# 512- and 256-column matmuls with added halves in the q, k and first gate and value units of an encoder block

## The chip, the core and the metric

The kernel runs on one NeuronCore of a Trainium2 chip. The metric is the device time of one execution in microseconds; of several runs the median is taken. The engines named below: PE is TensorE (matmul; PEld are its weight loads), DVE is VectorE, ACT is ScalarE, POOL is GpSimd, SP is SyncE, which issues most transfers.

## The reference

One layer of a bidirectional encoder, 256 positions of 2048 features, everything in float32:

```python
h = rmsnorm(x, norm1_g)
q, k, v, u = split(h @ w_in)             # 12 q heads, 4 k and v heads of 128, u 512 wide
a = window_attention(q, k, v, sink)      # |t-s| <= 128, ALiBi, a sink logit for each head
f = fourier_mix(u, w_fourier)            # DFT over positions and channels, then a map per group
x = x + concat(rmsnorm(a), rmsnorm(f)) @ w_out
h = rmsnorm(x, norm2_g)
gate, val = split(h @ w_up)              # 5504 each: 43 tiles of 128
gate = conv3(gate) + dw_b                # depthwise over positions
y = rmsnorm(x + (gelu(gate) * val) @ w_down)
```

## The kernel before

Every large product is made of three: an operand is split into a high part (rounded to fp32r, the form that PE multiplies fast) and a low part (what the rounding left), and high x high, high x low and low x high are summed in PSUM. Weights come by DMA into `raw`, and `split` makes the parts: ACT copies the high half into a tile `parts`, DVE subtracts for the low half (L170, L171). `parts` has three buffers; `PLACES` says how many columns into the tile the two halves start. A unit's weights are split two units ahead.

The work is a row of units, written out by hand in the order in which each engine runs it; there is no scheduler. First u and v (weights stream, the activations are stationary), then 16 units of k and q (`QK_ORDER`: one k head, its three q heads, four times), the output projection, then gate and value tiles in pairs (`ups`). In the q, k, gate and value units the weights are stationary: for each of 16 slices of the contraction `still_weights` runs three matmuls of 256 columns into the same 256 columns of a PSUM bank. Their moving operand is `hT[k // 4][:, k % 4, :]`, 512 columns: the activations' high part in the first 256 (`h[:, 0:S]`) and the low part behind it:

```python
for n, (w, o) in enumerate([(hi, 0), (hi, S), (lo, 0)]):
    nc.tensor.matmul(ps[:, 0:S], w[:, s], h[:, o : o + S], ...)
```

After a unit its PSUM is read: k is scaled by `r1b` on DVE, q is split straight from PSUM (`qk_out`, `qk_parts`); a gate or value tile is scaled by `r2b` (`scaled_sum`), the gate goes through the convolution and GELU, and both are multiplied. Around a q or k unit lie the small matmuls of heads further on: scores, transposes and values (`before` a unit on PE, `beside` and `behind` it on ACT, DVE and POOL).

Gate and value units of the first eight tiles, and three more, run one after another: 19 units, the first two of them interleaved with transposes of x. From then on (`PATTERN`) they alternate with products of the down-projection (`by_parts`: 12 matmuls of 512 columns each). The last six gate and value units again run on end, between two blocks of down units of 96 matmuls of 512 columns.

Of the kernel before, what the change touches and what calls it, by code (L numbers as in the profile page):

```python
# [8 lines left out]
F32 = mybir.dt.float32  # L9
F32R = mybir.dt.float32r  # L10
AF = mybir.ActivationFunctionType
ALU = mybir.AluOpType

P = 128
D = 2048
S = 256
NK = D // P
# [46 lines left out]
def ff_items():  # L64


    def ups(tiles):
        return [(kind, j) for j in tiles for kind in ("gate", "val")]

    items = ups(range(8))  # L70
    for g in range(N_GROUPS):
        todo = {
            "u": ups(range(8 * g + 8, 8 * g + 16)),
            "s": [("product", g, c, p) for c in range(2) for p in PRODUCTS[c]],
        }
        items += [todo[c].pop(0) for c in PATTERN]
        assert not any(todo.values())
    items += [("down", 0, c) for c in range(4)] + ups(LAST)
    items += [("down", 1, c) for c in range(4)] + [("last", c) for c in range(4)]
    return items  # L80
# [3 lines left out]
def block_kernel(  # L84
# [18 lines left out]
    nc = tc.nc  # L103
# [10 lines left out]
    def bank(pool, name):  # L114
        return pool.tile([P, 512], F32, tag=pool.name, name=name)


    units = [(w_in[i], 2048, "first" if i < N_QK else "still") for i in range(24)]
    units += [(w_out[i], 2048, "moving") for i in range(16)]
    n_front = len(units)  # L120
    items, up_index = ff_items(), {}
    for n, it in enumerate(items):
        if it[0] == "product":
            continue
        up_index[n] = len(units)
        if it[0] in ("gate", "val"):
            units.append((w_up[2 * it[1] + (it[0] == "val")], 2048, "still"))
        elif it[0] == "down":
            units.append((w_down_late[4 * it[1] + it[2]], 2048, "moving"))
        else:  # L130
            units.append((w_down_last[it[1]], 512 * len(LAST), "moving"))
    RAW = 3
    raws, halves = {}, {}


    PLACES = {"still": (0, 32), "first": (16, 16), "moving": (0, 0), "product": (28, 28)}

    def parts_tile(name, place):
        t = wp.tile([P, 2 * 2048 + 128], F32R, tag="parts", name=name, bufs=3)
        oh, ol = PLACES[place]  # L140
        return t[:, oh : oh + 2048], t[:, 2048 + ol : 4096 + ol]
# [38 lines left out]
    ph = pa.enter_context(tc.tile_pool(name="pa", bufs=1))  # L180

    hT = []
# [19 lines left out]
    first = load(0, 4)  # L202
# [50 lines left out]
    ps = bank(dn, "ps_warm")  # L253
# [58 lines left out]
                ps, ah, wl, start=False, stop=last and q == q0 + len(kk) - 1  # L312
            )

    def still_weights(hi, lo, ps, kk):


        for k in kk:
            h = hT[k // 4][:, k % 4, :]
            s = slice(k * P, (k + 1) * P)  # L320
            for n, (w, o) in enumerate([(hi, 0), (hi, S), (lo, 0)]):
                nc.tensor.matmul(  # L322
                    ps[:, 0:S], w[:, s], h[:, o : o + S],
                    start=k == 0 and n == 0, stop=k == NK - 1 and n == 2,
                )
# [17 lines left out]
    before, beside, behind = {}, {}, {}  # L343

    def at(when, i, f, *a):
        when.setdefault(i, []).append((f, a))
# [17 lines left out]
    for k in range(NK):  # L364
        c, q = k // 4, k % 4
# [4 lines left out]
        hi, lo = halves[c]  # L370
# [49 lines left out]
    r1b = ph.tile([P, S], F32, tag="r1b", name="r1b")  # L420
# [137 lines left out]
    for c in range(4):  # L558

        def work(hi, lo):  # L560
            for b in range(2):
                moving_weights(
                    hi, lo, 512, range(4 * c, 4 * c + 4), hk, b, ps_v[b], c == 0, c == 3
                )
# [4 lines left out]
    qk_sb, st = {}, {}  # L569
    sq_a = ph.tile([P, S], F32, tag="sq", name="sq_a")  # L570

    def qk_out(kind, h):
        ps = st.pop(("ps", kind, h))[:, 0:S]
        if kind == "k":
            add = ph.tile([P, S], F32, tag="add", name=f"add_{kind}{h}", bufs=2)
            nc.vector.tensor_tensor(add, ps, r1b, ALU.mult)
            ps = add
        st["add", kind, h] = ps

    def qk_parts(kind, h):  # L580

# [99 lines left out]
    for i in range(N_QK, N_OUT + 8):  # L681
        heads = {i - s: h for (kind, h), s in slot_of.items() if kind == "q"}
        new = [kh for kh, s in slot_of.items() if i - s == 1]
        if 5 in heads:
            at(before, i, values, heads[5])
        if 4 in heads:
            at(before, i, turn, heads[4])
        if 2 in heads:
            at(before, i, scores, heads[2])
        if 3 in heads:  # L690
            at(beside, i, weigh, heads[3])
        for kind, h in new:
            at(beside, i, qk_out, kind, h)
        if 5 in heads:
            at(beside, i, values_out, heads[5])
        if 4 in heads:
            at(beside, i, turn_out, heads[4])
        for kind, h in new:
            at(beside, i, qk_parts, kind, h)
        if 2 in heads:  # L700
            at(beside, i, scores_out, heads[2])
            at(behind, i, exps, heads[2])

    fourier_channels_steps()
    for n, (kind, h) in enumerate(QK_ORDER):

        def work(hi, lo):
            ps = st["ps", kind, h] = bank(mm, f"ps_{kind}{h}")
            still_weights(hi, lo, ps, range(NK))

        unit(N_QK + n, work)

# [49 lines left out]
    for n, (c, kq) in enumerate(OUT_ORDER):  # L762
        i = N_OUT + n
# [14 lines left out]
        if kq >= 2:  # L778
            part = "a" if kq == 2 else "f"
            ps = ps_a[c] if kq < 3 else ps_a[c, "f"]  # L780
# [15 lines left out]
    fp = ctx.enter_context(tc.tile_pool(name="fp", bufs=2))  # L796
    hT[:] = hT2
    r2b = fp.tile([P, S], F32, tag="r2b", name="r2b", bufs=1)
    parts = {}
    gate_out, sums_of, act = {}, {}, {}  # L800

    def scaled_sum(ps, name):
        add = fp.tile([P, S], F32, tag="fadd", name=f"fa_{name}", bufs=3)
        nc.vector.tensor_tensor(add, ps[:, 0:S], r2b, ALU.mult)  # L804
        sums_of[name] = add

    def gate_conv(j):
# [139 lines left out]

    def up_posts(n, kind, j, ps):
        if kind == "gate":
            at(beside, n + 1, scaled_sum, ps, f"g{j}")  # L950
            at(beside, n + 2, gate_conv, j)
            at(behind, n + 2, gate_gelu, j)
        else:
            at(beside, n + 1, scaled_sum, ps, f"v{j}")
            at(beside, n + 2, val_mult, j)
            if j % 8 == 7 and j < 8 * N_GROUPS:
                g = j // 8
                at(behind, n + 1, operand, g, "P1")
                at(behind, n + 2, operand, g, "N4")
                at(behind, n + 3, operand_sums, g, 0)  # L960
                at(behind, n + 4, operand, g, "P7")
                at(behind, n + 4, operand, g, "P2")
                at(behind, n + 5, operand_sums, g, 1)
                at(behind, n + 5, operand, g, "N5")
                at(behind, n + 6, operand, g, "N3")
                at(behind, n + 7, operand, g, "P6")
            if j >= 8 * N_GROUPS:
                at(behind, n + 2, act_parts, j)
# [102 lines left out]
    for q in range(2):  # L1071
        kind, j = items[q]
        ps = bank(mm, f"ps_{kind}{j}")
# [15 lines left out]
    for n, it in enumerate(items):  # L1089
        if n < 2:  # L1090
            continue
        if it[0] == "last":
            break
        if n in (8, 9):
            ring_load()
        if n == 13:
            pending.append(lambda: first_sums(0, 0))
        if it[0] in ("gate", "val"):
            kind, j = it
            ps = bank(mm, f"ps_{kind}{j}")  # L1100
            still_weights(*halves.pop(up_index[n]), ps, range(NK))
            ff_step(n)
            up_posts(n, kind, j, ps)
            continue
        if it[0] == "product":
            kind, g, c, p = it
            end = g == N_GROUPS - 1
            if (c, p) in held:
                by_parts(held[c, p], parts[p], *halves.pop(it), g == 0, end)
            else:  # L1110
                ps = bank(mm, f"ps_{p}{g}{c}")
                by_parts(ps, parts[p], *halves.pop(it), True, True)
                at(beside, n + 1, product_out, g, c, p, ps)
            if end and p == "N4":
                at(behind, n + 1, shared_out, c)
        else:
            kind, g, c = it
            hi, lo = halves.pop(up_index[n])
            ps = [bank(mm, f"ps_l{g}{c}{b}") for b in range(2)]
            for b in range(2):  # L1120
                moving_weights(hi, lo, 512, LATE[g], act.get, b, ps[b], True, True)
            at(beside, n + 1, down_out, c, ps)
            if (g, c) == (0, 0):
                gfb = fp.tile([P, D], F32, tag="sumw", name="gfb", bufs=1)
                nc.gpsimd.dma_start(gfb, normf_g.partition_broadcast(P))
        ff_step(n)
# [3 lines left out]
    i = up_index[n]  # L1130
# [145 lines left out]
```

## Time and profile before

| | before |
|---|---|
| median of 3 runs | 959.62 us (959.04 to 959.85) |
| the profiled execution | 959.13 us |
| its span, first to last instruction | 957.4 us |
| PE, weight loads | busy 947.8 and 884.8 us |
| DVE, ACT, POOL | busy 703.0, 510.5 and 44.6 us |
| HBM | 208.65 MB read, 2.10 MB written |

The span is the time between the first and the last instruction on the core; the execution's own time holds some 1.7 us around it. Matmuls are pipelined: a row's duration is that of one matmul from its first operand to its modelled end (277 ns for 256 columns), and the pace is the distance between starts. The row of the chain of work that ended last gives a start, a length and the number of matmuls that it merged.

### The profile page before, as it was taken

How to read it: one execution, taken by the hardware profiler on the slowest of the kernel's cores; microseconds unless marked ns; L12 is line 12 of the kernel's file. 1: busy time of each engine (PE TensorE's matmuls, PEld its weight loads, DVE VectorE, ACT ScalarE, POOL GpSimd, SP SyncE). 2: the span in 40 equal slices, each digit the busy share in tenths (PEclk: the TensorE clock that was granted, in tenths of full speed). 3: DMA queues.
4: the chain of work that ended last, by engine and by line, in shares of the span. 5: the costliest groups of instructions: out<-in, count | busy, mean ns of one | idle time of the engine just before them, and what ended most of it. 6: DMA issues, size and time to landing. Idle time of an engine off the chain costs nothing.

```text
span 957.4 us, 15831 instructions
## 1 busy us (share of the span) xinstructions
PE 947.8 (99%) x6721; PEld 884.8 (92%) x6721; DVE 703.0 (73%) x822; ACT 510.5 (53%) x552; POOL 44.6 (5%) x59
## 2 busy tenths in 40 slices
PE   9999999999999999999999999999999999999996
PEld 7799999888899999999999999999999999998985
DVE  5658766666566667786888877987778879787664
ACT  6855655544453346555555555554555655553433
POOL 0000000000000000000000000000000000000003
PEclk9999999999999999999999999999999999999998
DMA  8954444455555676879688798777987786775542
GB/s 322 340 195 164 161 138 157 151 176 186 196 181 197 253 224 209 231 248 301 205 270 251 232 293 264 234 251 221 285 256 249 218 292 200 242 246 211 177 132 88
DMA packets 33558, 211.77 MB, mean 221 GB/s; under 512 B 3792, under 2 KB 4304, under 8 KB 9424
## 3 DMA queue, kind: packets, MB, share of 16 engines
q1 hardware_dynamic: 29744, 184.54, 52.8%
q0 software_dynamic: 3600, 26.22, 14.7%
q8 instruction: 52, 0.85, 0.3%
q14 instruction: 18, 0.15, 0.1%
q10 hardware_dynamic: 144, 0.01, 0.0%
HBM read 208.65 MB, written 2.10 MB: 220 GB/s over the span
## 4 chain that ended last, share of the span: by engine, by line
PE 96%; DMA 2%; ACT 0%; DVE 0%; issue 0%; POOL 0%; ACTq 0%; POOLq 0%; SPq 0%
PE ps_gate L322 25%; PE ps_val L322 25%; PE ps_q L322 7%; PE ps_P L1010 3%; PE ps_P L1011 3%; PE ps_P L1012 3%; PE ps_k L322 2%; PE ps_a L311 2%; PE ps_a L309 2%; PE ps_a L310 2%; PE ps_N L1010 2%; PE ps_N L1012 2%; PE ps_N L1011 2%; DMA raw<-in_w_in 2%; PE ps_l L309 2%; PE ps_l L310 2%
## 5 line engine op out<-in xcount | busy, mean ns | idle before, releaser
L171 DVE TENSOR_TENSOR parts<-raw,parts 128x2048 fp32r<-128x2048 f32 (+3 forms) x145 | 313.1, 2159 | 76.7 <-ACT parts L170 76.3
L170 ACT ACTIVATE parts<-raw 128x2048 fp32r<-128x2048 f32 (+3 forms) x144 | 262.4, 1823 | 170.4 <-PE ps_val L322 40.0
L322 PEld LDWEIGHTS ps_gate<-hU,parts 128*128 128x128 f32 x2064 | 242.6, 188 | 2.3
L322 PE MATMUL ps_gate<-hU,parts 128*128 128x256 f32 x2064 | 244.5, 277 | 0.0
L322 PEld LDWEIGHTS ps_val<-hU,parts 128*128 128x128 f32 x2064 | 242.1, 188 | 2.2
L322 PE MATMUL ps_val<-hU,parts 128*128 128x256 f32 x2064 | 244.1, 277 | 0.0
L322 PE MATMUL ps_q<-hT,parts 128*128 128x256 f32 x576 | 69.5, 279 | 0.0
L322 PEld LDWEIGHTS ps_q<-hT,parts 128*128 128x128 f32 x576 | 67.9, 188 | 0.0
L1011 PE MATMUL ps_P<-parts_P,op_P 128*128 128x512 f32 x128 | 49.8, 389 | 0.0
L1010 PE MATMUL ps_P<-parts_P,op_P 128*128 128x512 f32 x128 | 49.8, 389 | 0.0
L1012 PE MATMUL ps_P<-parts_P,op_P 128*128 128x512 f32 x128 | 49.8, 389 | 0.0
L906 ACT ACTIVATE parts_N<-sumw 128x2048 fp32r<-128x2048 f32 x16 | 30.7, 1917 | 35.7 <-PE ps_val L322 22.5
L907 DVE TENSOR_TENSOR parts_N<-sumw,parts_N 128x2048 fp32r<-128x2048 f32 x16 | 36.6, 2289 | 16.8 <-ACT parts_N L906 16.8
L309 PE MATMUL ps_a<-parts,cat 128*128 128x512 f32 x96 | 37.9, 395 | 0.0
L311 PE MATMUL ps_a<-parts,cat 128*128 128x512 f32 x96 | 37.5, 390 | 0.0
L310 PE MATMUL ps_a<-parts,cat 128*128 128x512 f32 x96 | 37.3, 389 | 0.0
L1010 PE MATMUL ps_N<-parts_N,op_N 128*128 128x512 f32 x96 | 37.3, 389 | 0.0
L1011 PE MATMUL ps_N<-parts_N,op_N 128*128 128x512 f32 x96 | 37.3, 389 | 0.0
L1012 PE MATMUL ps_N<-parts_N,op_N 128*128 128x512 f32 x96 | 37.3, 389 | 0.0
L804 DVE TENSOR_TENSOR fa_g<-ps_gate,r2b 128x256 f32<-128x256 f32 x43 | 18.1, 422 | 23.1 <-PE ps_gate L322 23.1
L1012 PEld LDWEIGHTS ps_P<-parts_P,op_P 128*128 128x128 f32 x128 | 24.0, 188 | 5.0
L906 ACT ACTIVATE parts_P<-sumw 128x2048 fp32r<-128x2048 f32 x8 | 15.3, 1917 | 23.1 <-PE ps_gate L322 13.2
(307 smaller groups left out, 1267.3 us busy)
## 6 DMA issues: line engine op xcount, KB each, us to landing
raw<-in_w_up SPq DMA_DIRECT2D x86, 1024.0 KB, 5.4
raw<-in_w_in SPq DMA_DIRECT2D x21, 1024.0 KB, 4.9
raw<-in_w_out SPq DMA_DIRECT2D x16, 1024.0 KB, 4.8
sumw<-in_w_down POOLq DMA_DIRECT2D x16, 1024.0 KB, 8.8
raw<-in_w_down_late SPq DMA_DIRECT2D x8, 1024.0 KB, 5.0
raw<-in_w_down_last SPq DMA_DIRECT2D x4, 768.0 KB, 4.3
raw<-in_w_in SPq DMA_DIRECT2D x8, 256.0 KB, 6.2
xs<-in_x SPq DMA_DIRECT2D x4, 512.0 KB, 10.1
```

What stands on the lines that cost most here:

```text
L170: nc.scalar.activation(hi[:, s], raw[:, s], AF.Copy)
L171: nc.vector.tensor_tensor(lo[:, s], raw[:, s], f32(hi[:, s]), ALU.subtract)
L309: nc.tensor.matmul(ps, ah, wh, start=first and q == q0, stop=False)
L310: nc.tensor.matmul(ps, al, wh, start=False, stop=False)
L311: nc.tensor.matmul(ps, ah, wl, start=False, stop=last and q == q0 + len(kk) - 1)
L322: nc.tensor.matmul(ps[:, 0:S], w[:, s], h[:, o : o + S], start=k == 0 and n == 0, stop=k == NK - 1 and n == 2,)
L804: nc.vector.tensor_tensor(add, ps[:, 0:S], r2b, ALU.mult)
L906: nc.scalar.activation(hi, src, AF.Copy)
L907: nc.vector.tensor_tensor(lo, src, f32(hi), ALU.subtract)
L1010: nc.tensor.matmul(ps, o[:, 0, p, :], hi[:, s], start=first and p == 0, stop=False)
L1011: nc.tensor.matmul(ps, o[:, 1, p, :], hi[:, s], start=False, stop=False)
L1012: nc.tensor.matmul(ps, o[:, 0, p, :], lo[:, s], start=False, stop=last and p == 3)
```

## The change

The q and k units, and the 19 gate and value units ahead of the first product, get another form of the same three terms. One matmul of 512 columns takes the high weights against both halves of the activations, so that high x high lands in the first 256 columns of the bank and high x low in the second; one matmul of 256 columns adds low x high to the first. The halves are added afterwards: ACT copies the second half out of PSUM, DVE adds it to the first. In the q and k units, and in the third gate or value unit, the high matmuls run up to five slices ahead of the low ones (`lag=4`). The low half of the weights starts 16 columns into its tile in these units, not 32. Gate and value units from the first product on keep three matmuls of 256 columns and the old place; their function is now called `still_thirds`, their place `thirds`.

```diff
+    FIRST_PRODUCT = min(n for n, it in enumerate(items) if it[0] == "product")
...
         if it[0] in ("gate", "val"):
-            units.append((w_up[2 * it[1] + (it[0] == "val")], 2048, "still"))
+            form = "still" if n < FIRST_PRODUCT else "thirds"
+            units.append((w_up[2 * it[1] + (it[0] == "val")], 2048, form))
...
-    PLACES = {"still": (0, 32), "first": (16, 16), "moving": (0, 0), "product": (28, 28)}
+    PLACES = {"still": (0, 16), "thirds": (0, 32), "first": (16, 16), "moving": (0, 0), "product": (28, 28)}
...
-    def still_weights(hi, lo, ps, kk):
-        for k in kk:
+    def still_weights(hi, lo, ps, kk, lag=0):
+        todo = [("hi", k) for k in kk[: lag + 1]]
+        for n, k in enumerate(kk):
+            todo.append(("lo", k))
+            todo += [("hi", q) for q in kk[lag + 1 + n : lag + 2 + n]]
+        for part, k in todo:
+            h = hT[k // 4][:, k % 4, :]
+            s = slice(k * P, (k + 1) * P)
+            if part == "hi":
+                nc.tensor.matmul(ps, hi[:, s], h, start=k == 0, stop=False)
+            else:
+                nc.tensor.matmul(
+                    ps[:, 0:S], lo[:, s], h[:, 0:S], start=False, stop=k == NK - 1
+                )
+
+    def still_thirds(hi, lo, ps):
+        for k in range(NK):
             h = hT[k // 4][:, k % 4, :]
             s = slice(k * P, (k + 1) * P)
             for n, (w, o) in enumerate([(hi, 0), (hi, S), (lo, 0)]):
...
-    def qk_out(kind, h):
-        ps = st.pop(("ps", kind, h))[:, 0:S]
+    def qk_out(kind, h, ps):
+        tmp = ph.tile([P, S], F32, tag="tmp", name=f"tmp_{kind}{h}", bufs=2)
+        nc.scalar.activation(tmp, ps[:, S : 2 * S], AF.Copy)
+        add = ph.tile([P, S], F32, tag="add", name=f"add_{kind}{h}", bufs=2)
+        nc.vector.tensor_tensor(add, ps[:, 0:S], tmp, ALU.add)
         if kind == "k":
-            add = ph.tile([P, S], F32, tag="add", name=f"add_{kind}{h}", bufs=2)
-            nc.vector.tensor_tensor(add, ps, r1b, ALU.mult)
-            ps = add
-        st["add", kind, h] = ps
+            nc.vector.tensor_tensor(add, add, r1b, ALU.mult)
+        st["add", kind, h] = add
...
-            still_weights(hi, lo, ps, range(NK))
+            still_weights(hi, lo, ps, range(NK), lag=4)
...
-    def scaled_sum(ps, name):
+    def scaled_sum(ps, name, whole):
         add = fp.tile([P, S], F32, tag="fadd", name=f"fa_{name}", bufs=3)
-        nc.vector.tensor_tensor(add, ps[:, 0:S], r2b, ALU.mult)
+        if whole:
+            nc.vector.tensor_tensor(add, ps[:, 0:S], r2b, ALU.mult)
+            sums_of[name] = add
+            return
+        tmp = fp.tile([P, S], F32, tag="ftmp", name=f"ft_{name}")
+        nc.scalar.activation(tmp, ps[:, S : 2 * S], AF.Copy)
+        nc.vector.tensor_tensor(add, ps[:, 0:S], tmp, ALU.add)
+        nc.vector.tensor_tensor(add, add, r2b, ALU.mult)
         sums_of[name] = add
...
-            at(beside, n + 1, scaled_sum, ps, f"g{j}")
+            at(beside, n + 1, scaled_sum, ps, f"g{j}", n >= FIRST_PRODUCT)
...
-            still_weights(*halves.pop(up_index[n]), ps, range(NK))
+            if n < FIRST_PRODUCT:
+                still_weights(*halves.pop(up_index[n]), ps, range(NK), lag=4 if n == 2 else 0)
+            else:
+                still_thirds(*halves.pop(up_index[n]), ps)
```

More of the change, by code (lines that the diff above doesn't have):

```diff
@@ L692, in block_kernel @@
         for kind, h in new:
-            at(beside, i, qk_out, kind, h)
+            at(beside, i, lambda k=kind, h=h: qk_out(k, h, st.pop(("ps", k, h))))
         if 5 in heads:
@@ L953, in up_posts @@
         else:
-            at(beside, n + 1, scaled_sum, ps, f"v{j}")
+            at(beside, n + 1, scaled_sum, ps, f"v{j}", n >= FIRST_PRODUCT)
             at(beside, n + 2, val_mult, j)
```

## The prediction

> **What bounds the kernel now.** I read the page first, then the list of waits for TensorE (PE), then the chain that ended last in order of time, then the timeline of PE alone around the places where the chain changes its pace.
>
> ```profile
> span 957.4 us, 15831 instructions
> PE 947.8 (99%) x6721; PEld 884.8 (92%) x6721; DVE 703.0 (73%) x822; ACT 510.5 (53%) x552; POOL 44.6 (5%) x59
> ```
>
> ```profile
> PE ps_warm L255 <- POOL ones L247: 1.0, 1, 1.0
> PE ps_u L309 <- ACT parts L170: 0.2, 1, 0.2
> ```
>
> PE is busy from end to end and in the whole program waits 1.2 us for another engine, all of it in the first stage. So a change counts only by what it does to PE's own stream, or if it makes PE wait where it does not now. The question is then how fast PE gets through its matmuls, and the busy share can't say that. The chain can: each row is one unit of 48 matmuls (16 slices of the contraction, three matmuls of 256 columns each).
>
> ```profile
> 57.39 5.47 PE ps_k L322 x48
> 63.31 5.47 PE ps_q L322 x48
> 69.22 5.48 PE ps_q L322 x48
> 75.85 5.71 PE ps_q L322 x48
> 82.27 5.71 PE ps_k L322 x48
> 89.12 5.47 PE ps_q L322 x48
> 96.08 5.56 PE ps_q L322 x48
> 103.50 5.71 PE ps_q L322 x48
> 110.64 5.45 PE ps_k L322 x48
> 117.24 5.46 PE ps_q L322 x48
> 123.85 5.71 PE ps_q L322 x48
> 131.41 5.71 PE ps_q L322 x48
> 138.55 5.45 PE ps_k L322 x48
> 145.16 5.46 PE ps_q L322 x48
> 151.76 5.70 PE ps_q L322 x48
> 159.33 5.71 PE ps_q L322 x48
> 273.56 5.70 PE ps_gate L322 x48
> 364.87 5.71 PE ps_gate L322 x48
> 373.35 5.45 PE ps_val L322 x48
> 422.32 5.44 PE ps_val L322 x48
> 876.79 5.71 PE ps_gate L322 x48
> ```
>
> There are two paces for the same 48 matmuls. The fast one is 5.44 us, 113.3 ns a matmul; the slow one is 5.71 us, 119 ns. Of the 16 q and k units 7 are slow and 9 are fast or nearly so. Once products lie between the units (from 373 us) they are fast; the six after the products (876.79 is the first) are slow again. The 17 units from 273.32 to 370.41 us are all slow, which the second row here shows: 97.09 us are 17 times 5.71.
>
> ```profile
> 110.47:138.39 27.92, 27.92 (x243) 27.92 (x241) 20.15 (x46) 16.87 (x32) 2.21 (x3) 1.00 0.45 152
> 273.32:370.41 97.09, 97.09 (x819) 97.09 (x818) 63.92 (x69) 42.55 (x39) 1.05 (x1) 1.00 0.65 218
> ```
>
> (Columns: stretch, its length, then busy time of PE, weight loads, DVE, ACT, POOL with their counts; granted clock; DMA share; GB/s.) The granted clock is 1.00 in both, so the slow pace is no throttle. DVE and ACT have a third of each stretch free or more.
>
> What do 512 columns cost? The timeline of PE at the first products has both paces:
>
> ```profile
> 370.41 0.40 PE L1010 MATMUL ps_P<-parts_P,op_P 128*128 128x512 f32 x1
> ...
> 371.34 0.40 PE L1011 MATMUL ps_P<-parts_P,op_P 128*128 128x512 f32 x1
> 371.58 0.39 PE L1012 MATMUL ps_P<-parts_P,op_P 128*128 128x512 f32 x1
> ...
> 373.19 5.61 PE L322 MATMUL ps_val<-hU,parts 128*128 128x256 f32 x48
> 378.64 0.39 PE L1010 MATMUL ps_P<-parts_P,op_P 128*128 128x512 f32 x1
> ...
> 381.36 5.60 PE L322 MATMUL ps_gate<-hU,parts 128*128 128x256 f32 x48
> ```
>
> From 378.64 to 381.36 twelve matmuls of 512 columns take 2.72 us, 226.7 ns each: exactly twice 113.3. At the fast pace time is columns and nothing else, so 512 + 256 columns cost what three times 256 cost, 340 ns, and the change gains nothing where units are fast already. The twelve just before, from 370.41 to 373.19, follow slow units and take 2.78 us, 231.7 ns each: 5 ns more a matmul, about the same surplus as the 5.6 ns of the slow 256 columns, on twice the columns. So the slow pace looks like a price for each matmul, not for each column. And it is left there: the unit after those twelve (373.35) is fast, and everything behind it.
>
> **The change, part by part.** (1) Thirty-five units change their matmuls: 16 of q and k, 19 of gate and value. In each, the two matmuls of 256 columns with the high weights become one of 512, the third stays at 256. That removes 560 matmuls and 560 weight loads and no columns. At the fast pace a unit costs 16 x 340 ns = 5.44 us as before.
>
> What could be gained is therefore the slow surplus of today. Seven q and k units at 0.26 us are 1.8 us; 17 gate and value units at 0.27 are 4.6 us; and the first pair, whose first part runs from
>
> ```profile
> 260.97 4.45 PE L322 MATMUL ps_gate<-hU,parts 128*128 128x256 f32 x36
> 265.26 1.04 PE L744 MATMUL ps_x<-ident,xs 128*128 128x128 f32 x8
> ```
>
> 260.97 to 265.26, 4.29 us for 36 matmuls that are 4.08 at the fast pace, has 0.2. The sum is 6.6 us. It is the most that the matmuls of these units can give, and the largest term by far.
>
> How much of it goes? No place of this trace alternates 512 and 256 columns within a unit, so it is bounded. From above in gain: all 35 units fast, 6.6 us. From below: each matmul keeps its slow price in all 35 units, 5.0 ns for a 512 and 5.6 for a 256, 10.6 ns a slice where three slow ones have 16.8; 16 slices in 35 units make 5.9 us in place of 6.6, a gain of 0.7. Below nothing: the worst single step of 512 columns above is from 371.34 to 371.58, 0.24 us, 13 ns over the fast one; were every pair as bad, 13 + 5.6 = 19 ns a slice would be 10.4 us, 3.8 more than now.
>
> I take a value near the upper end. The row nearest to the new units is the passage at 370.41, slow units followed by 512 columns, and there the pace is fast again after the twelve. A 256-column matmul also leaves its weight load hardly room: loads are busy 97.09 us of the 97.09 in the slow stretch. In the changed unit a load lies under 512 columns every other time. So I count the 4.8 us of gate and value in full, where nothing interrupts the units, and half of the 1.8 of q and k, where transposes and score matmuls lie between the units and the pace is found anew each time: 5.7 us, less 0.1 for such entries into units that are fast already: 5.6 us.
>
> The Trainium skill, "TensorE: Matmul & The Clock Gate", Back-to-back issue gap, gives N/2.4 + 2.5 ns for an isolated matmul of N columns. By it the fixed 2.5 ns would be saved 560 times, an estimate of 1.4 us, in any state. The trace disagrees with a fixed term at the fast pace (226.7 is twice 113.3), and shows a larger one at the slow pace.
>
> (2) The halves have to be added. Each of the 35 units gets one ACT copy of 128x256 out of PSUM and one DVE addition with an operand in PSUM. The nearest rows:
>
> ```profile
> L262 ACT ACTIVATE qT<-ps_q 128x256 fp32r<-128x256 f32 x11 | 4.3, 387 | 6.8 <-PE ps_q L322 6.8
> L804 DVE TENSOR_TENSOR fa_g<-ps_gate,r2b 128x256 f32<-128x256 f32 x9 | 3.8, 423 | 7.3 <-PE ps_gate L322 7.3
> ```
>
> So 35 x 0.39 = 13.6 us of ACT and 35 x 0.42 = 14.8 us of DVE. In the four units from 110.47 to 138.39 DVE goes from 20.15 to 21.8 of 27.9 us and ACT from 16.87 to 18.4; in the gate stretch DVE from 63.92 to 71 of some 92.5. Both keep 20% free. The copy waits for its unit's last matmul; behind it on ACT stand the outputs of the attention heads and then the high half of the weights two units on, and DVE's addition stands ahead of that unit's low half. Their slack:
>
> ```profile
> 285.01 1.92 ACT L170 ACTIVATE parts<-raw 128x2048 fp32r<-128x2048 f32 x1 [1.56 <-PE ps_val L322]
> 286.96 2.29 DVE L171 TENSOR_TENSOR parts<-raw,parts 128x2048 fp32r<-128x2048 f32 x1 [1.52 <-ACT parts L170]
> ```
>
> The split that starts with the third of the 17 units (273.32 and twice 5.71 is 284.7) is done at 289.25 and is used two units on, at 296 us: 7 us of slack against some 0.8 us of delay. I cost the additions at nothing on the path; their cover is that slack, and if it were gone PE would wait up to 0.8 us a unit. The order of high matmuls five slices ahead of the low ones (16 q and k units, one gate unit) gives the low half 1.1 us more still; no unit waits for it today, so it is worth nothing.
>
> (3) The low half lies 16 columns into its tile in these 35 units where it was 32. I see no row that prices an offset; it belongs to the unknown of (1). The units after the first product are issued as before. The transfers keep their order and start a few us earlier; the DMA share of 0.65 rises by a twentieth at most.
>
> **The sum.** The profiled execution took 959.13 us for a span of 957.4; 959.13 - 5.6 = 953.5. The median of the three runs is 0.5 above that execution, so I forecast 954.0.
>
> **The rivals.**
> *A price for each matmul remains.* All 35 units stay slow at 10.6 ns a slice: 0.7 us gained, 958.9. For it: the slow pace held through 17 units on end. Against it: 512 columns left it within a dozen. The fixed term of the page named above would come out in the same place, 958.2.
> *The mixed stream has a slow pace of its own.* The high weights of the next slice must now be loaded under the only 256-column matmul of a slice, while the 512 columns read both halves of the activations; if that order settles at steps like the worst ones seen, 0.24 us and 0.119 us, the units cost 5.44 + 0.30 us each, the time grows by 3.8 us to 963.4. It decides from 12 ns a slice on (6.6 us over 560 slices), that is where a changed unit takes over 5.63 us. For it: the pace of this kernel plainly depends on what streams follow one another (876.79 is slow straight behind fast 512-column matmuls). Against it: every long run of 512 columns in the trace ended fast.
> *The additions come too late.* Scores of a head would wait for its q. With 20% of DVE free I see no more than 3 in 100; at 0.4 us for each of 12 heads it would eat the gain, to 959.
>
> **How the numbers follow.** A measurement of this kernel tells about 0.2%, 1.9 us, from no change. The forecast, most units fast, gets 0.58: its own range is 952.2 (all 6.6 us, and some 0.8 for the score and value matmuls between the q and k units: 144 of them at 5.6 ns) to 957.6. A price that remains, and the late additions, lie within 0.2% and get 0.17 + 0.03. The slow mixed stream gets 0.22. The range goes from 952.2 to 962.0: it takes in the first three and the milder half of the last. Faster 0.58, same 0.20, slower 0.22.
>
> **What would show it.** In the chain after, changed units (now 32 matmuls) at 5.44 us, above all the 17 behind the pair: then the stage from 273 to 370 is 92.5 us long. At 5.61 the price for each matmul remains; above 5.63 the mixed stream is worse. PE's list of waits should stay at 1.2 us; a row of ACT or DVE from these units in it would show late additions. I am wrong if the 17 units keep 97 us or more, or if the stages behind the first product change their pace.

## The result, and the profile after

The changed kernel takes 954.2 us (median of 4 runs, 953.55 to 955.03) against 959.51 (median of 4, 959.04 to 959.85): a ratio of 0.9945, 95% interval 0.9928 to 0.9963. The forecast was 954.0. The page of the execution of 953.55 us:

```profile
span 951.8 us, 14812 instructions
PE 941.9 (99%) x6161; PEld 856.8 (90%) x6161; DVE 717.3 (75%) x857; ACT 522.2 (55%) x587; POOL 44.5 (5%) x59
```

PE has 560 instructions fewer and is still busy end to end. DVE has 14.3 us more work, ACT 11.7. PE's list of waits after the change:

```profile
PE ps_warm L257 <- POOL ones L249: 1.0, 1, 1.0
PE ps_u L311 <- ACT parts L172: 0.6, 1, 0.6
```

Both are in the first stage, as before; no wait came from the added copies and additions. Next the busy times by stretch: first all q and k units with what lies between them, then the gate and value units up to the first product, then four q and k units, then the 17 gate and value units alone.

```profile
57.33:165.48 108.15, 108.15 (x687) 97.73 (x686) 84.63 (x191) 70.41 (x136) 8.10 (x11) 1.00 0.44 156
260.13:364.92 104.79, 104.79 (x621) 92.91 (x620) 76.33 (x96) 54.12 (x66) 1.74 (x2) 1.00 0.65 221
110.39:137.94 27.55, 27.55 (x179) 25.00 (x177) 21.99 (x51) 18.57 (x36) 2.21 (x3) 1.00 0.44 156
272.31:364.92 92.61, 92.61 (x547) 82.00 (x546) 70.72 (x86) 47.55 (x57) 1.05 (x1) 1.00 0.66 227
```

Before, the first two stretches were 109.15 us (57.15 to 166.30) and

```profile
260.97:370.41 109.44, 109.44 (x925) 109.44 (x924) 69.52 (x79) 49.13 (x48) 1.74 (x2) 1.00 0.63 213
```

109.44. So 4.65 us came from gate and value, 1.00 from q and k. The first stage was 0.18 us longer, everything else is the same within 0.1 us; the spans differ by 5.6. The value units of the 17 by form, with shortest, median and longest duration:

```profile
L328 PE MATMUL ps_val<-hU,parts x128: 389/389/389, 277.9 to 359.1; 128*128 128x512 f32 x128
L330 PE MATMUL ps_val<-hU,parts x128: 276/276/276, 278.1 to 359.4; 128*128 128x256 f32 x128
```

Every matmul of these units has the duration of the fast pace. The last six gate and value units, which the change leaves alone, are as slow as before:

```profile
876.91 5.71 PE ps_val L341 x48
```

The total is as forecast. Whether for the forecast's reason was open: the change alters the form of the matmuls, their order, the place of the low half and what is added, and the argument rested on the form alone.

### The profile page after: what moved, and what is told of

Same layout as the page of the kernel before. It is cut to its first block, busy times and chain, and to the rows that moved or that the text cites. A ratio compares the mean times of both kernels' runs of the same rounds, so it can differ in the third digit from the quotient of the medians.

```text
span 951.8 us, 14812 instructions
## 1 busy us (share of the span) xinstructions
PE 941.9 (99%) x6161; PEld 856.8 (90%) x6161; DVE 717.3 (75%) x857; ACT 522.2 (55%) x587; POOL 44.5 (5%) x59
## 4 chain that ended last, share of the span: by engine, by line
PE 96%; DMA 2%; DVE 0%; ACT 0%; POOL 0%; issue 0%; ACTq 0%; POOLq 0%; SPq 0%
PE ps_val L341 20%; PE ps_gate L341 19%; PE ps_q L328 5%; PE ps_gate L328 4%; PE ps_val L328 3%; PE ps_P L1039 3%; PE ps_P L1037 3%; PE ps_P L1038 3%; PE ps_q L330 2%; PE ps_a L313 2%; PE ps_a L311 2%; PE ps_a L312 2%; PE ps_N L1039 2%; PE ps_N L1037 2%; PE ps_N L1038 2%; DMA raw<-in_w_in 2%
## 5 line engine op out<-in xcount | busy, mean ns | idle before, releaser
L341 PEld LDWEIGHTS ps_val<-hU,parts 128*128 128x128 f32 x1632 | 190.3, 188 | 2.2
L341 PE MATMUL ps_val<-hU,parts 128*128 128x256 f32 x1632 | 191.3, 276 | 0.0
L341 PEld LDWEIGHTS ps_gate<-hU,parts 128*128 128x128 f32 x1584 | 184.9, 188 | 2.2
L341 PE MATMUL ps_gate<-hU,parts 128*128 128x256 f32 x1584 | 185.7, 276 | 0.0
L328 PE MATMUL ps_q<-hT,parts 128*128 128x512 f32 x192 | 61.3, 393 | 0.0
L328 PE MATMUL ps_gate<-hU,parts 128*128 128x512 f32 x160 | 54.6, 390 | 0.0
L328 PE MATMUL ps_val<-hU,parts 128*128 128x512 f32 x144 | 49.6, 390 | 0.0
L330 PE MATMUL ps_q<-hT,parts 128*128 128x256 f32 x192 | 45.5, 278 | 0.0
L330 PE MATMUL ps_gate<-hU,parts 128*128 128x256 f32 x160 | 43.6, 276 | 0.0
L328 PEld LDWEIGHTS ps_q<-hT,parts 128*128 128x128 f32 x192 | 35.2, 188 | 6.8
L330 PE MATMUL ps_val<-hU,parts 128*128 128x256 f32 x144 | 39.8, 276 | 0.0
L1037 PE MATMUL ps_N<-parts_N,op_N 128*128 128x512 f32 x96 | 37.3, 389 | 0.0
```

Source lines behind the costliest of these rows:

```text
L328: nc.tensor.matmul(ps, hi[:, s], h, start=k == 0, stop=False)
L330: nc.tensor.matmul(ps[:, 0:S], lo[:, s], h[:, 0:S], start=False, stop=k == NK - 1)
L341: nc.tensor.matmul(ps[:, 0:S], w[:, s], h[:, o : o + S], start=k == 0 and n == 0, stop=k == NK - 1 and n == 2,)
L1037: nc.tensor.matmul(ps, o[:, 0, p, :], hi[:, s], start=first and p == 0, stop=False)
```

## The experiments

The stretch from the first gate matmul to the first product ("gate stage") is the measure in most of them. It does not depend on the first stage, which began its hand-over to k at 56.9 to 58.6 us in the profiles of all kernels and moves single times by over 1 us. The first nine experiments were executed once each, so their total times are single ones; the last three have 4 or 5 runs. The stage lengths are steadier: the gate stage is 104.79 us in the changed kernel's profile and again in those of five experiments below that leave its first three units as they are.

**The place alone.** On the kernel before:

```diff
-    PLACES = {"still": (0, 32), ...
+    PLACES = {"early": (0, 16), "still": (0, 32), ...   # early: the 35 units
```

> The kernel before, with one thing changed: in the 35 early units the low half of the weights starts 16 columns into its tile, as in the changed kernel; matmuls, and no added halves, as before. Theory M (the price is one for each matmul, and the 512-column form lets PE leave the slow pace): the 17 units behind the first pair stay at 5.71 us each, time within 1 us of the kernel before. Rival P (the place of the low half sets the pace): the 17 units run at 5.44 us and the time falls by 4 to 6 us, to about 954.

959.99 us; gate stage

```profile
262.57:371.30 108.73, 108.73 (x926) 108.73 (x924) 69.40 (x78) 49.10 (x48) 1.74 (x2) 1.00 0.63 214
```

and a unit of the 17 in the chain:

```profile
281.01 5.65 PE ps_val L324 x48
```

Neither theory's pace: the place does change it, from 5.71 to 5.65, and the units do not become fast. The time is within 1 us of the kernel before, as Theory M had it, but as a balance: the gate stage is 0.7 us shorter, and the q and k stage takes 110.61 us where it took 109.15, since all 16 of its units are slow now.

**The form alone.** On the changed kernel:

```diff
-    PLACES = {"still": (0, 16), "thirds": (0, 32), ...
+    PLACES = {"still": (0, 32), "thirds": (0, 32), ...
```

> The changed kernel, with the low half back at 32 columns into its tile in the 35 units. Theory M: the 17 units keep 5.44 us, time about 954. Rival P: they go back towards 5.6 us or more (price for each matmul), time 957 to 959.

958.16 us; gate stage, and the value units of the 17 by form:

```profile
261.06:369.48 108.42, 108.42 (x622) 93.98 (x620) 76.69 (x96) 53.94 (x66) 1.74 (x2) 1.00 0.61 214
```

```profile
L328 PE MATMUL ps_val<-hU,parts x128: 394/397/398, 279.0 to 363.5; 128*128 128x512 f32 x128
L330 PE MATMUL ps_val<-hU,parts x128: 278/278/279, 279.3 to 363.7; 128*128 128x256 f32 x128
```

The 512-column matmuls take 397 ns where they took 389, on end for 17 units. The units take 5.65 us. Theory M, the forecast's, falls: 512 columns do not lead PE out of the slow pace by themselves. Of the 4.65 us this kernel keeps 1.0.

**The count alone.** On the changed kernel, everything else kept:

```diff
-                nc.tensor.matmul(ps, hi[:, s], h, start=k == 0, stop=False)
+                for o in (0, S):
+                    nc.tensor.matmul(
+                        ps[:, o : o + S], hi[:, s], h[:, o : o + S],
+                        start=k == 0 and o == 0, stop=False,
+                    )
```

> The changed kernel, with each matmul of 512 columns cut into two of 256 (the same weights, the same two halves of the bank, the same order, place and additions). It isolates the count of matmuls from everything else of the change. Theory M: the slow pace is back, 17 units at 5.71 us, time 958 to 960. Rival (place, order or the two halves of the bank set the pace): 5.44 us and about 954. If the added halves cost anything on the path, it shows here as a time above that of the kernel before; I expect none.

960.44 us; gate stage

```profile
263.05:371.79 108.74, 108.74 (x925) 108.74 (x924) 76.69 (x96) 53.99 (x66) 1.74 (x2) 1.00 0.62 213
```

The 17 units run at 5.65 us, not at the 5.71 that Theory M expected. The time is 0.9 us above the kernel before, which the expectation had named as the sign of a cost of the additions. The stages show that it is none: the gate stage is that of the place alone (108.73) with 7.3 us more of DVE and 4.9 more of ACT in it, and the q and k stage takes 110.69 us against 110.61 there, both 1.5 more than in the kernel before. So at 16 columns the 512-column form is needed, and with the form the 16 columns are. The gate stage by form and place (the right column has the five high matmuls ahead in the third unit, the left column has not; cut_512, which has them with 256 columns at 16, gives 108.74):

| low half at | three of 256 | 512 and 256 |
|---|---|---|
| 32 | 109.44 | 108.42 |
| 16 | 108.73 | 104.79 |

**Other places.** One kernel has the weights of all still units, also between the products, at 28 columns in both halves, in the form before; two vary the changed kernel.

```diff
-    PLACES = {"still": (0, 32), ...      # the kernel before
+    PLACES = {"still": (28, 28), ...     # still_28
-    PLACES = {"still": (0, 16), ...      # the changed kernel
+    PLACES = {"still": (16, 32), ...     # shift_both
+    PLACES = {"still": (0, 0), ...       # no_gap
```

> The kernel before, with both halves of the weights of every q, k, gate and value unit 28 columns into their tiles, as the product units have them, where they were at 0 and 32. Three matmuls of 256, nothing added. Two runs so far say that neither the form nor the place alone gives the fast pace (5.65 us a unit with either), both together do (5.44). Theory A (the pace follows from where the two streams of weights lie): the 17 units may run at any of 5.44 to 5.71 us here, and it is the same pace in the units between the products. Theory B (a run of units keeps the pace in which it is entered, the stream ahead of it decides): the 17 units stay slow, 5.65 to 5.71, since the same output projection stands ahead, and units between products stay at 5.44.

> The changed kernel, with both halves of the weights 16 columns further into the tile in the 35 units: 16 and 32 in place of 0 and 16. The distance between the halves is kept, the distance to the activations is not. If the distance between the two halves of the weights decides: 17 units at 5.44 us, time 954. If the place against the activations, or each by itself, decides: another pace, 5.5 to 5.65, time 955 to 958.

> The changed kernel, with the low half at 0 columns into its tile, as the high one, in the 35 units. Low half at 16: 5.44 us a unit; at 32: 5.65. If what counts is that the low half lies 16 columns (64 bytes) off the high one modulo 32 columns: 5.65 here as at 32, time 957 to 958.5. If the pace varies in another way with the place, it is 5.44 to 5.6.

still_28 took 974.81 us. The 17 units run at 5.68, which fits both theories, and the units between products, fast in every other kernel, are slow:

```profile
383.12 5.65 PE ps_gate L322 x48
391.50 5.66 PE ps_val L322 x48
```

So at this place units are slow even behind products. That speaks for theory A on those units; their stage, products included, is 14.5 us longer. shift_both took 956.87, gate stage 106.76; no_gap 959.56, gate stage 108.59. The distance between the halves is not all that counts, since (16, 32) keeps it and loses 2.0 us, at 5.55 us a unit. Low halves at 0 and at 32 are alike in the gate stage (108.59, 108.42), as that expectation's first case has it, though the time missed its 957 to 958.5: the q and k stage takes 110.13 us where form_only has 109.27. Two points do not make a period.

**What stands ahead.** On the changed kernel, the weights of the eight late down units, which come ahead of the last six gate and value units, in the place of the products:

```diff
-            units.append((w_down_late[4 * it[1] + it[2]], 2048, "moving"))
+            units.append((w_down_late[4 * it[1] + it[2]], 2048, "product"))
```

> The changed kernel, with the weights of the eight late down units placed 28 columns into their tiles, as those of the products, where they were at 0. So the last six gate and value units (three matmuls of 256, 5.71 us each so far) stand behind 512-column matmuls that differ from before in the place alone. Theory B (the stream ahead decides; behind products the same units run at 5.44): the six go to 5.44 us, time 952.6. Theory A (their own place and form decide): 5.71 us still, 954.

953.14 us. In the chain the six units, their form and place untouched, now run

```profile
872.40 5.45 PE ps_gate L341 x48
877.86 5.44 PE ps_val L341 x48
...
899.62 5.44 PE ps_val L341 x48
```

Theory B holds for them: with three of 256 at (0, 32) both paces can last for six units, and what stands ahead decides. It isn't that a pace is handed on, though. The timeline of this kernel up to the first of the six:

```profile
871.32 0.39 PE L313 MATMUL ps_l<-parts,act 128*128 128x512 f32 x1
871.55 0.39 PE L311 MATMUL ps_l<-parts,act 128*128 128x512 f32 x1
871.78 0.40 PE L312 MATMUL ps_l<-parts,act 128*128 128x512 f32 x1
872.02 0.39 PE L313 MATMUL ps_l<-parts,act 128*128 128x512 f32 x1
872.24 0.97 PE L341 MATMUL ps_gate<-hU,parts 128*128 128x256 f32 x7
```

Three steps of 512 take 0.70 us there, slow, and fast units follow; with the old place the steps were fast (870.14 to 870.82, 0.68 us) and slow units followed.

**The entry to the gate stage.** If the entry decides there as well, the 17 units need no new form but in the first of them:

```diff
-    FIRST_PRODUCT = min(n for n, it in enumerate(items) if it[0] == "product")
+    FIRST_PRODUCT = 3
```

> The changed kernel, with the new form kept in the q and k units and in the first three gate and value units alone; the 16 behind them, up to the first product, have three matmuls of 256 again, low half at 32, nothing added: just what ran at 5.71 us a unit in the kernel before, but now entered from units that run fast. Theory B (at this place two paces are possible, and the one in which a run is entered lasts): the 16 run at 5.44 us, time about 954, and the additions of 16 units are not needed. Theory A (without 512 columns these units fall back to the slow pace by themselves): 5.71 us, 16 x 0.27 = 4.3 us more, 958.4.

954.93 us; gate stage, and the 16 units alone:

```profile
261.36:366.15 104.79, 104.79 (x877) 102.85 (x876) 70.29 (x81) 50.04 (x51) 1.74 (x2) 1.00 0.65 221
279.11:366.15 87.04, 87.04 (x770) 87.04 (x769) 59.42 (x67) 40.14 (x37) 1.05 (x1) 1.00 0.70 237
```

```profile
279.27 5.44 PE ps_val L341 x48
```

104.79 us, to the hundredth that of the changed kernel, with the very matmuls that took 5.71 us before. Weight loads are busy for all of the 87.04 us, at the fast pace: loads that fill the stretch are no sign of the slow one.

Fast matmuls ahead are not enough by themselves. In the kernel before, the last four slices of each unit of the first pair ran at the fast pace, 1.36 us for 12 matmuls from start to start, and only four matmuls of 128 columns lay between them and the third unit, which ran slow (273.56 in the chain, 5.70 us):

```profile
270.23 1.52 PE L322 MATMUL ps_gate<-hU,parts 128*128 128x256 f32 x12
271.59 1.53 PE L322 MATMUL ps_val<-hU,parts 128*128 128x256 f32 x12
```

So it is the third unit itself that settles on a pace, and the 16 behind it keep it.

**The order at the entry.** The high matmuls five slices ahead, taken away:

```diff
-            still_weights(hi, lo, ps, range(NK), lag=4)          # q and k
+            still_weights(hi, lo, ps, range(NK))
-                still_weights(*..., ps, range(NK), lag=4 if n == 2 else 0)
+                still_weights(*..., ps, range(NK), lag=0)
```

> The changed kernel, with each low matmul directly behind its high one in the q and k units and the third gate or value unit (no five high ones ahead). No unit waits for its low half in the changed kernel, so the waits of PE stay as they are. If the order among the matmuls matters to the pace only at the entry to a unit, the gate stage is unchanged (104.8 us from its first matmul to the first product) and the q and k stage moves by no more than 0.16 us a unit: 953 to 956.

956.53 us; gate stage 107.46, 2.67 more. The third unit, the first of the 17, now settles slow, and the 16 behind it stay so at 5.60 us. The 512-column matmuls of the value units from 280 to 360 us (busy us, then the mean duration in ns, 389 at the fast pace):

```profile
L328 PE MATMUL ps_val<-hU,parts 128*128 128x512 f32 x118 | 41.7, 395 | 0.0
```

The expectation of an unchanged gate stage was wrong, and the time lies above its 953 to 956; the q and k stage moved by 0.2 us alone (108.35). An order that hides no wait was worth 2.7 us. That unit three, the entry to 16 others, is where it counts, and not the q and k units, follows from three_units below, which keeps the order in unit three alone.

The order is not enough without the place. In the changed kernel and in form_only the five high matmuls at the head of the third unit go alike, 1.24 us from the first of them to the first low one. Behind that the changed kernel runs at 340 ns a slice and form_only at some 347: they part where the low half, at its other place, comes in.

**Versions that go further.** The last six in the new form (`form = "still" if n < FIRST_PRODUCT or it[1] in LAST`), or both entries mended (`FIRST_PRODUCT = 3` and the late downs at "product"), or the latter with q and k back in the form of before:

> The changed kernel, with the last six gate and value units (871 to 905 us, all slow at 5.71 us there) in the 512 and 256 form too, halves added, low half at 16 columns. Theory M: they go to 5.44 us, 6 x 0.27 = 1.6 us less, time about 952.6. Rival (the pace of a run of units is set by what streams stand ahead of it, here 96 matmuls of 512 columns of the down units, whatever the form): 5.6 to 5.71 us and no gain, 954.

> The changed kernel with both entries mended: new form in the q and k units and the first three gate and value units alone (as entry_only), and the late down units' weights 28 columns into their tiles (as late_place). If the pace is kept from the entry, both gains stand together: gate stage 104.8 us, the last six units at 5.44 us; 1.4 us less than the changed kernel at the same first stage, 952.4 to 953.

> As entry_late, with the q and k units back in the form and place of the kernel before (three of 256, low half at 32, nothing added). Only three units of the whole kernel have the new form. If the gate stage depends on its own entry alone, it stays at 104.8 us and the last six at 5.44; q and k take 109.15 us in place of 108.15, so 1.0 us more than entry_late, 953.5 to 954. If the pace there came from what the q and k units leave, it falls back to 109.4 and the time is about 958.

| | median us | ratio to the kernel before | q and k | gate stage |
|---|---|---|---|---|
| last_six | 952.36 | 0.9927 (0.9910 to 0.9943) | 108.15 | 104.79 |
| entry_late | 952.83 | 0.9928 (0.9914 to 0.9941) | 108.15 | 104.79 |
| three_units | 953.89 | 0.9938 (0.9925 to 0.9950) | 109.65 | 104.79 |

The medians of the first two lie 1.8 and 1.4 us below the changed kernel's, but the intervals of the ratios overlap its own (0.9928 to 0.9963); that they gain rests on the last six units, at 5.44 us in both profiles. The two can't be told from each other; entry_late gets there with fewer additions. three_units shows that the gate stage does not depend on q and k. Its q and k stage missed by 0.5 us: nine of the 16 units are slow where seven were,

```profile
90.06 5.71 PE ps_q L341 x48
97.25 5.81 PE ps_q L341 x48
```

these two in addition, with the same matmuls in the same order as in the kernel before. So the pace of a q or k unit is open to something that differs between programs or executions; what, no run tells.

## Why the prediction was right, and where not

*What bounds the kernel.* Right: PE's stream alone, with PE's waits at 1.2 us before and 1.6 after.

*The size.* Forecast 4.8 us from gate and value, 0.9 from q and k; measured 4.65 and 1.00. The 17 units behind the pair take 92.61 us, where 92.5 was named as the sign. The 1.00 is a balance: the q and k units that were slow now take 5.49 to 5.57 us from start to start, while the first three, at 5.55 before, take 5.58 to 5.69.

*Step (1), the mechanism.* Wrong as it was put. "512 columns left it within a dozen" was read off one passage, where the weights lay at another place, and the passage doesn't show it: with the row

```profile
371.80 0.39 PE L1010 MATMUL ps_P<-parts_P,op_P 128*128 128x512 f32 x1
```

the first six of the twelve take 1.39 us (370.41 to 371.80) and the last six 1.39 (to 373.19). They are slow to the end; it is the unit behind them, three of 256, that runs fast. With the low half at 32 the same form stays slow for 17 units on end: 5.65 us, just the rival's mark ("above 5.63 the mixed stream is worse"), and the q and k stage of that kernel is 109.27 us, worse than before. The rival of a slow pace of the mixed stream was therefore real, one offset away. Without the order the units ran at 5.60, where the prediction put 5.61 for a price that remains. And most of the slow surplus is no price for each matmul: where both forms are slow at the same place, 16 matmuls fewer save 0.05 to 0.06 us a unit (5.71 to 5.65 at 32, 5.65 to 5.60 at 16) of a surplus of 0.27 and 0.21. What the change bought is not fewer such prices, it is a stream in which the fast pace holds.

*Step (2), the additions.* Right: no wait, DVE 21.99 us (21.8 forecast) in four q and k units and 70.72 (71) in the 17; and cut_512 has them all without a cost in its stages. But the order of the high matmuls was put at nothing, since it hid no wait, and is worth 2.7 us.

*Step (3), the place.* Left in the unknown of (1) because no row priced it. With the form and the order there it carried 3.6 us of the gate stage (108.42 to 104.79), with the form of before 0.7. An edit that no row prices should have had its own chance of spoiling the forecast.

*The late additions* did not occur. The fixed 2.5 ns for a matmul, by the Trainium skill ("TensorE: Matmul & The Clock Gate", Back-to-back issue gap), gave an estimate of 1.4 us. form_only, which has that saving with the old place, is 1.0 us shorter in the gate stage and 0.1 longer in q and k. At the fast pace the traces show no fixed term: a unit of 48 matmuls (entry_only) and one of 32 (the changed kernel) both take 5.44 us.

So the number was right by the size of what could be gained, and the cause was half right. That the gain came in full was in part luck: it hung on the place, which the forecast left unpriced, and on the order, which it put at nothing. With the low half left at 32 the gate stage gained 1.0 us, and without the order 2.0, not 4.65. Shown: changed as they were, the units need form, place and order together to run fast; changing the first three gate and value units alone gives all of the gate stage's gain, and behind them the old form at the old place runs fast too; additions are free. Not shown: whether the new form at 32 columns would run fast behind a third unit that is fast, and why a place or an entry gives one pace or the other.

## What to carry to other kernels

A busy PE can still have paces: take starts, not durations, divide a unit's length by its columns, and compare equal units in different surroundings before costing a change of form. Where two paces exist, look at how a run is entered first: mending the entry of a run (a few units, an offset of the weights ahead of it, an order of matmuls) gave as much here as changing all of it. Test an offset, a form and an order one at a time: in the gate stage the offset alone was worth 0.7 us, the form with the order 1.0, the form with the offset 2.0, and all three 4.65.

## What was not expected of the hardware

A stationary operand's offset in its tile moved the pace. Units between products, three of 256, run at 113.3 ns a matmul with the halves at (0, 32) and at about 118 with both at 28 (still_28). With the low half at 32 in place of 16, the 512-column matmuls of the 17 units, whose own weights did not move, went from 226.7 ns to about 236 (form_only). At one offset (0, 32) the same 48 matmuls ran at 5.44 us a unit (entry_only, late_place) or 5.71 (the kernel before) for as long as the run lasted, according to what stood ahead of it; PE's list shows no wait there, and the granted clock was 1.00 in both.
